# One access order for the products of a hybrid decoder trunk: parts and blocks of the tokens read in turn, with a PSUM layout to match

## The chip, the cores and the metric

The kernel runs on one core of a Trainium2 chip. The metric is the time of one execution in device microseconds; the kernel before takes 815.08 us, the median of three runs that lie between 813.9 and 815.81 us. A profile records one execution, instruction by instruction, on the engines of the core: TensorE (PE, with its weight loads listed apart as PEld), VectorE (DVE), ScalarE (ACT), GpSimd (POOL) and SyncE (SP), and the transfers of the DMA engines.

## The reference

Two layers work on 256 tokens of width 1024. Each layer normalises the stream, multiplies it by one wide input projection, runs three token mixers (a state-space scan, a sliding-window attention, a forgetting attention), gates and projects their outputs, merges them, and adds the result of an output projection to the stream. Cut to what matters here:

```python
for layer in range(DEPTH):
    h = rms_norm(x, norm_w[layer])                       # (256 tokens, 1024)
    proj = jnp.einsum('bsd,de->bse', h, w_in[layer])     # all branches from one projection
    (a_xbc, a_z, a_dt, b_q, b_k, b_v, b_z,
     c_q, c_k, c_v, c_f, c_z, gates) = jnp.split(proj, split_at, axis=-1)
    y_a = mamba2_branch(a_xbc, a_z, a_dt, ...)           # conv, scan, gate, group norm
    y_b = sliding_window_branch(b_q, b_k, b_v, b_z, ...)
    y_c = forgetting_attention_branch(c_q, c_k, c_v, c_f, c_z, ...)
    branch = jnp.einsum('bsiw,iwd->bsid', jnp.stack([y_a, y_b, y_c], axis=2), w_proj[layer])
    g = jax.nn.sigmoid(gates.reshape(b, s, N_BRANCH, d) + gate_bias[layer])
    x = x + jnp.einsum('bsd,de->bse', jnp.sum(g * branch, axis=2), w_out[layer])
return rms_norm(x, final_norm_w)
```

Everything is float32. The change touches how the columns of `proj` are computed that the kernel wants with channels on partitions: `a_xbc`, `a_z`, `b_q`, `b_k`, `b_z`, `c_q`, `c_k` and `c_z`.

## The kernel before, in words

**Two parts for each number.** TensorE multiplies values of a shortened float type (`F32R`). To keep float32 accuracy each operand is split into a high part, the value rounded to that type, and a low part, the rest. Weights arrive by DMA as parts of 1024 words a partition (`raw`), and `split` (L293 on ScalarE, L294 on VectorE) makes `hi` and `lo` of each. The tokens of a layer, normalised and transposed, are held in one tile `y.hT` of shape [128, 2, 2, 8, 128] (made in `both_streams`, L1226): the first 2 is the part `h` (high or low), the second is the block `a` of 128 tokens, then come the eight slices `k` of the width of 1024, then the 128 tokens `i` of a block. In words of four bytes, neighbouring tokens are 1 apart, the two blocks 1024 apart, the two parts 2048 apart. `y.hTh` and `y.hTl` are the high and the low part of it.

**The products that the change touches** are made by `both_sums`. It computes 128 channels by 256 tokens into `p`, one PSUM tile of 512 float32 columns (one of three with the name `mm`). For each of eight slices k there are two matmuls, both with weights as the stationary operand: the 512-wide product of the weights' high part with both parts of the tokens, and the 256-wide product of the weights' low part with the high part of the tokens. (The product of the two low parts is left out.) The first one writes columns 0 to 511: high tokens go to columns 0 to 255, low tokens to 256 to 511. The second one adds to columns 0 to 255. Within each half the two blocks of tokens alternate: token i of block a is column 2i + a. This order, which the kernel calls "in turn" (`tokens_in_turn`, `in_turn`), is used for the moving operand of every F32R matmul; where the weights are the moving operand (`tok`, `tok2`, `u_proj_normed`, with `dense`), the two halves of a row of weights alternate in the same way.

**After the products** the two halves of `p` have to be added, which also undoes the order (`ordered`, `halves`). `dma_sum` evicts both with ScalarE (L489, L490), and a DMA on GpSimd's queue (L491) adds one to the other in SBUF. `chan_sum` evicts the low half with ScalarE (L481) and adds the high half with VectorE (L482). There are 132 such calls: 84 `dma_sum` and 48 `chan_sum`.

**The order of the work** is written by a small planner at build time: `mm` adds an estimate for each matmul by its number of columns to a clock of its own, and `pump` uses this clock to decide where pieces of attention and scan are put between the products. The matmuls on TensorE then run in that written order. All matmuls are issued by one line, L109, and all transposes by L113, so groups are told apart by the names of tiles: `mm<-L,hi` is the 512-wide product of `both_sums` and `mm<-L,lo` the 256-wide one (L is a tile of tokens, hi and lo are the weights' parts), while `mm<-hi,L` and `mm<-lo,L` are the products in which the weights move.

Of the kernel before, what the change touches and what calls it, by code (L numbers as in the profile page):

```python
# [13 lines left out]
AF = mybir.ActivationFunctionType  # L14
ALU = mybir.AluOpType

P = 128
S = 256
# [32 lines left out]
def hybrid_trunk(  # L51
# [17 lines left out]
    def T(tag, shape, dtype=F32, bufs=None):  # L69
        count[0] += 1  # L70
        return sb.tile(shape, dtype, tag=tag, name=f"{tag}_{count[0]}",
                       bufs=bufs if bufs is not None else BUFS.get(tag, 1))

    def PS(tag, bufs):
        count[0] += 1
        return ps.tile([P, 512], F32, tag=tag, name=f"{tag}_{count[0]}", bufs=bufs)

    def pmm():
        return PS("mm", 3)

    def pmx():
        return PS("mx", 5)

    act = nc.scalar.activation
    stt = nc.vector.scalar_tensor_tensor
    tt = nc.vector.tensor_tensor
# [16 lines left out]
    def mm(o, a, b, **kw):  # L103
        n = b.free_size()
        if a.dtype == F32R:
            clock["t"] += max(0.094, n / 2350.0)
        else:
            clock["t"] += max(0.2, n / 587.0) * (0.5 if a.free_size() == 64 or a.shape[0] == 32 else 1.0)
        nc.tensor.matmul(o, a, b, **kw)  # L109
# [166 lines left out]
    def tokens_in_turn(a, k):  # L276
        return a[:, :, k, :].rearrange("p a i -> p i a")

    def ordered(ap):

        return ap.rearrange("p (i a) -> p a i", a=2)

    def halves(ap):

        return ap.rearrange("p (a i) -> p a i", a=2)
# [21 lines left out]
    def dense(pt, ah, al, bh, bl, w, mid=None):  # L307

        for k in range(NK):
            for i, (a, b) in enumerate(((ah, bh), (al, bh), (ah, bl))):  # L310
                mm(pt, a(k), b(k), start=(k == 0 and i == 0), stop=(k == NK - 1 and i == 2))
            if w.last and (k + 1) % w.kper == 0:
                release(w, k // w.kper + 1)
            if mid is not None and k == NK // 2 - 1:
                mid()
# [90 lines left out]
    def release(w, n):  # L406
        if n > w.released:
            state["held"] -= n - w.released
            w.released = n
            feed()  # L410
# [17 lines left out]
    for l in range(L):  # L428
        y = Layer()
# [36 lines left out]
            nc.gpsimd.tensor_copy(y.dsk[r, :], y.hb[r, 64:80].rearrange("p (j i) -> p i j", i=2)[:, i, :])  # L466


    def chan(y, w, c):

        p = pmm()
        dense(p[:, 0:S], lambda k: w.hi(k)[:, c:c + P], lambda k: w.lo(k)[:, c:c + P],
              lambda k: tokens_in_turn(y.hTh, k), lambda k: tokens_in_turn(y.hTl, k), w)
        return ordered(p[:, 0:S])

    def chan_sum(y, w, c, out):


        p = pmm()
        both_sums(y, w, c, p)  # L480
        finish(act(halves(out), ordered(p[:, S:2 * S]), AF.Copy))  # L481
        tt(halves(out), ordered(p[:, 0:S]), halves(out), op=ALU.add)  # L482

    def dma_sum(y, w, c, out):

        p = pmm()
        both_sums(y, w, c, p)
        lo = T("L1", [P, S])
        act(halves(lo), ordered(p[:, S:2 * S]), AF.Copy)  # L489
        last = act(halves(out), ordered(p[:, 0:S]), AF.Copy)  # L490
        nc.gpsimd.dma_start(out, lo, accum_op=ALU.add)  # L491
        finish(last)

# [2 lines left out]
        ends_later.append(f if n == 1 else lambda: after_evictions(n - 1, f))  # L496

    def both_sums(y, w, c, p):
        for k in range(NK):
            if k > 0:  # L500
                mm(p[:, 0:S], w.lo(k)[:, c:c + P], tokens_in_turn(y.hTh, k), start=False, stop=False)
            mm(p, w.hi(k)[:, c:c + P], y.hT[:, :, :, k, :].rearrange("p h a i -> p h i a"),
               start=(k == 0), stop=(k == NK - 1))
            if k == 0:
                mm(p[:, 0:S], w.lo(k)[:, c:c + P], tokens_in_turn(y.hTh, k), start=False, stop=False)
            if w.last and (k + 1) % w.kper == 0:
                release(w, k // w.kper + 1)

# [33 lines left out]
    def rotated(y, done):  # L542

        held = {}

        def u(half):
            def f(w):
                p = T("L1", [P, S])
                dma_sum(y, w, half * P, p)

                def turned():
                    for i in (half, 1 - half):
                        m = held[half, i] = T("L1", [P, S])
                        tt(m, p, cs[:, i, :], op=ALU.mult)
                    if half == 1:
                        done(held)
                after_evictions(3, turned)
                pump()
            return f
        return u(0), u(1)  # L560
# [253 lines left out]
    def u_conv(y, u, c):  # L814
        def f(w):
            if u == 8:
                y.bcT = T("L8", [P, 8, S])
            if u == 0:
                y.xs = T("L8", [P, 8, S])
            dst = y.xs[:, u, :] if u < 8 else y.bcT[:, u - 8, :]  # L820
            x_ = T("L1", [P, S])
            dma_sum(y, w, c, x_)

            def taps():
                a = T("L1", [P, S])
                act(a, x_, AF.Identity, scale=y.vec[:, 48 + u:49 + u], bias=y.vec[:, 64 + u:65 + u])  # L826
                for j in (2, 1, 0):
                    s = 3 - j
                    stt(a[:, s:S], x_[:, 0:S - s], y.vec[:, 16 * j + u:16 * j + u + 1], a[:, s:S],  # L829
                        op0=ALU.mult, op1=ALU.add)  # L830
                ends_later.append(lambda: end(a))

            def end(a):
                th = T("L1", [P, S])
                act(th, a, AF.Tanh)  # L835
                stt(dst, th, 1.0, a, op0=ALU.add, op1=ALU.mult)
                if u < 8 and u % 2 == 1:
                    launch(0, ssd_group(y, u // 2), D_G0)
            after_evictions(3, taps)
            pump()  # L840
        return f
# [4 lines left out]
    def finish(out):  # L846

        with tc.issue_after(out.ins):
            for _ in range(len(ends_later)):
                ends_later.pop(0)()  # L850
# [67 lines left out]
    def u_z(y, br, u, c):  # L918
        def f(w):
# [12 lines left out]
            if br == 1:  # L932
                dma_sum(y, w, c, o)
                after_evictions(3, gated)
                pump()
                return
            chan_sum(y, w, c, o)

            def normed():
# [88 lines left out]
    def u_ck(y, j, c):  # L1028
        def f(w):
            y.ckT[j] = T("qt", [P, 2, S])  # L1030
            (dma_sum if j < EARLY else chan_sum)(y, w, c, y.ckT[j][:, 0, :])
            if j % 2 == 0:
                launch(2, fox_quad(y, j), D_FOX)
            pump()
        return f

    def u_cq(y, j, c):
        def f(w):
            (dma_sum if j < EARLY else chan_sum)(y, w, c, y.ckT[j][:, 1, :])
            y.cqdone[j] = clock["t"] + (D_ADD if j < EARLY else 0.0)  # L1040
            pump()
        return f
# [210 lines left out]
    for y in layers:  # L1253
        l = y.l
        w = w_in[l]
# [149 lines left out]
    with tc.manual_schedule(engines={ENG.PE, ENG.DVE, ENG.Activation, ENG.Pool}):  # L1405
# [11 lines left out]
        p = pmx()  # L1417
# [93 lines left out]
        for i in range(2):  # L1511
# [6 lines left out]
                                op=ALU.add)  # L1518
# [50 lines left out]
```

## Time and profile before

| what | value |
|---|---|
| median of three runs | 815.08 us (813.9 to 815.81) |
| the profiled execution | 813.07 us, of which the span from first to last instruction is 811.4 us |
| granted TensorE clock | 0.998 of full speed |
| PE, matmuls in flight | 800.2 us, 99% of the span |
| DVE | 683.8 us, 84% |
| ACT | 533.4 us, 66% |
| POOL | 172.7 us, 21% |
| 512-wide products of `both_sums` | 1056 |
| 256-wide products of `both_sums` | 1056 |

How to read the views: a duration of a matmul is the time from its start until it has left the array, and matmuls overlap, so what one costs in a stream is the distance between the starts of two. The chain of waits follows the work that ended last back from the end; a row of it with "x72" is a run of 72 instructions on one engine, each of which waited for nothing but the one before it, and the time of such a row divided by its count is the cost of one. In a row of a group, the number of partitions and elements stands behind the names, then the count, the busy time, the mean duration in ns and the idle time of the engine ahead of it.

### The profile page before, as it was taken

The numbers are of one execution on the slowest core, as the hardware profiler recorded it, in microseconds if no ns is written. First come the engines' busy times: TensorE is split into PE (matmuls) and PEld (weight loads), VectorE is DVE, ScalarE is ACT, GpSimd is POOL, SyncE is SP. The second block draws the span as 40 slices with busy tenths as digits, with TensorE's granted clock in tenths as the row PEclk, the third lists the DMA queues.
The fourth block names the chain that finished last, engine by engine and source line by source line (L and its number), as shares of the span: only waits on it lengthen the run. The fifth ranks groups of instructions, "written<-read, shape, count | busy, mean of one in ns | idle before, by whom it ended". The sixth has DMA issues, their size and how long they took to land.

```text
span 811.4 us, 14867 instructions
## 1 busy us (share of the span) xinstructions
PE 800.2 (99%) x5178; PEld 714.2 (88%) x5178; DVE 683.8 (84%) x1412; ACT 533.4 (66%) x1142; POOL 172.7 (21%) x227
## 2 busy tenths in 40 slices
PE   8999999999999999999999999999999999999996
PEld 8998988888888888888998899888888988888896
DVE  6869999978998998776775799999879989869865
ACT  7777767865875785543565678677747677745452
POOL 3167113130321000130001741122313410002000
PEclk9999999999999999999999999999999999999999
DMA  9998888699675565667688987689986645566632
GB/s 311 279 262 183 240 221 203 197 261 252 175 211 163 164 191 180 211 208 246 214 261 259 241 209 220 159 214 257 272 253 175 212 130 160 172 228 218 210 106 77
DMA packets 139418, 170.43 MB, mean 210 GB/s; under 512 B 9976, under 2 KB 107072, under 8 KB 139344
## 3 DMA queue, kind: packets, MB, share of 16 engines
q1 hardware_dynamic: 114960, 140.53, 55.9%
q0 software_dynamic: 12928, 12.68, 9.8%
q10 hardware_dynamic: 11456, 16.28, 7.1%
q8 instruction: 41, 0.67, 0.3%
q14 instruction: 33, 0.27, 0.1%
HBM read 154.71 MB, written 2.16 MB: 193 GB/s over the span
## 4 chain that ended last, share of the span: by engine, by line
PE 96%; DMA 2%; DVE 1%; ACT 1%; issue 0%; SPq 0%; DVEq 0%
PE mm L109 83%; PE mx L109 10%; PE mx L113 3%; DMA raw<-in_w_in_dram 1%; DMA raw<-in_w_proj_dram 1%; DMA hb<-in_sinks_dram 0%; DVE lo L294 0%; ACT L L695 0%; ACT hi L293 0%; SPq L363 0%; SPq L189 0%; DVE L L1431 0%; DVE L L1127 0%; DVE L L1128 0%; ACT L L1435 0%
## 5 line engine op out<-in xcount | busy, mean ns | idle before, releaser
L109 PE MATMUL mm<-L,hi 128*128 128x512 f32 x1056 | 354.6, 387 | 0.3
L294 DVE TENSOR_TENSOR lo<-raw,hi 128x1024 fp32r<-128x1024 f32 (+1 forms) x276 | 313.1, 1153 | 37.8 <-ACT hi L293 36.6
L109 PE MATMUL mm<-hi,L 128*128 128x512 f32 (+2 forms) x1168 | 303.3, 349 | 0.1
L293 ACT ACTIVATE hi<-raw 128x1024 fp32r<-128x1024 f32 (+1 forms) x276 | 265.6, 981 | 51.1 <-PE mm L109 37.1
L109 PE MATMUL mm<-L,lo 128*128 128x256 f32 x1056 | 266.6, 273 | 0.0
L109 PEld LDWEIGHTS mm<-hi,L 128*128 128x128 f32 x1168 | 206.0, 190 | 22.6 <-issue 1.0
L109 PEld LDWEIGHTS mm<-L,hi 128*128 128x128 f32 x1056 | 195.2, 190 | 28.0 <-issue 5.2
L109 PEld LDWEIGHTS mm<-L,lo 128*128 128x128 f32 x1056 | 202.1, 191 | 5.3
L109 PE MATMUL mm<-lo,L 128*128 128x512 f32 (+2 forms) x584 | 201.5, 347 | 0.0
L109 PEld LDWEIGHTS mm<-lo,L 128*128 128x128 f32 x584 | 110.2, 190 | 10.7
L491 POOL DMA_DIRECT2D L<-L x68 | 60.1, 908 | 198.2 <-ACT L L490 153.8
L1057 POOL TENSOR_SCALAR_AFFINE_SELECT bias<-bias 128x128 f32<-128x128 f32 x64 | 40.7, 671 | 69.3 <-DMA bias<-cumd 69.2
L829 DVE SCALAR_TENSOR_TENSOR L<-L,vec,L 128x255 f32<-128x255 f32 (+2 forms) x96 | 46.2, 481 | 2.1 <-ACT L L826 0.3
L489 ACT ACTIVATE L<-mm 128x256 f32<-128x256 f32 x84 | 32.1, 382 | 19.1 <-PE mm L109 15.6
L1091 ACT ACTIVATE L<-L 128x512 f32<-128x512 f32 x24 | 15.1, 631 | 39.9 <-DVE L L1088 31.7
L655 ACT ACTIVATE pp<-pp,nm 128x128 f32<-128x128 f32 x64 | 28.2, 442 | 18.3 <-DVE nm L649 18.3
L613 ACT ACTIVATE pp<-pp,nm 128x128 f32<-128x128 f32 x32 | 12.6, 394 | 25.1 <-DVE nm L618 24.4
L1088 DVE TENSOR_TENSOR L<-mm,L 128x512 f32<-128x512 f32 x22 | 15.1, 686 | 16.4 <-DMA L<-in_gate_bias_dram 8.8
L491 POOL DMA_DIRECT2D qt<-L x16 | 13.8, 860 | 70.9 <-ACT qt L490 69.4
L1124 POOL TENSOR_TENSOR L<-L,L 128x512 f32<-128x512 f32 x8 | 12.8, 1600 | 68.0 <-DVE L L1123 46.2
L490 ACT ACTIVATE L<-mm 128x256 f32<-128x256 f32 x68 | 26.3, 386 | 1.5 <-DMA L<-L 1.5
L835 ACT ACTIVATE L<-L 128x256 f32<-128x256 f32 x32 | 13.4, 418 | 19.0 <-DVE L L829 18.9
(210 smaller groups left out, 913.7 us busy)
## 6 DMA issues: line engine op xcount, KB each, us to landing
raw<-in_w_in_dram SPq DMA_DIRECT2D x191, 512.0 KB, 5.3
raw<-in_w_proj_dram SPq DMA_DIRECT2D x48, 512.0 KB, 5.6
L<-L POOLq DMA_DIRECT2D x72, 128.0 KB, 5.1
raw<-in_w_out_dram SPq DMA_DIRECT2D x16, 512.0 KB, 4.8
bias<-cumd ACTq DMA_DIRECT2D x16, 256.0 KB, 3.7
L<-cumd ACTq DMA_DIRECT2D x8, 512.0 KB, 5.4
L<-in_gate_bias_dram ACTq DMA_DIRECT2D x12, 256.0 KB, 6.2
qt<-L POOLq DMA_DIRECT2D x16, 128.0 KB, 5.5
```

The lines of the kernel that those rows point to most:

```text
L109: nc.tensor.matmul(o, a, b, **kw)
L113: nc.tensor.transpose(o, a, i)
L293: keep(act)(hi, src, AF.Copy)
L294: keep(tt)(lo, src, hi.bitcast(F32), op=ALU.subtract)
L489: act(halves(lo), ordered(p[:, S:2 * S]), AF.Copy)
L490: last = act(halves(out), ordered(p[:, 0:S]), AF.Copy)
L491: nc.gpsimd.dma_start(out, lo, accum_op=ALU.add)
L655: act(pp[:, i, sl], pp[:, i, sl], AF.Exp, scale=-1.0, bias=nm[:, e:e + 1], accum_out=sums[:, e:e + 1])
L829: stt(a[:, s:S], x_[:, 0:S - s], y.vec[:, 16 * j + u:16 * j + u + 1], a[:, s:S], op0=ALU.mult, op1=ALU.add)
L1057: nc.gpsimd.affine_select(out=bias[:, i, dst], in_=bias[:, i, src], compare_op=ALU.is_ge, fill=NEG, base=0, pattern=[[-1, P]], channel_mul ...
L1088: tt(halves(g), p, halves(y.gb), op=ALU.add)
L1091: finish(act(g, g, AF.Tanh, scale=0.5))
```

## The change

The 512-wide product reads the tokens in another order and so fills PSUM in another order. Before, it walks part, then token, then block (h, i, a): three nested steps. Now it walks token, then part and block together (i, then h and a), and since the part step of 2048 words is twice the block step of 1024, the four (h, a) combinations are one step of 1024 words taken four times: two nested steps. Token i of block a in part h is now column 4i + 2h + a of `p`. The 256-wide product reads what it read, and its result has to be added to the columns of the high part: it now writes columns 4i and 4i + 1, skips 4i + 2 and 4i + 3, and so on (`own`). The evictions read every fourth column, where they read every second one (`streams` in place of `ordered`). An unused function (`chan`) goes. Count, sizes and order of the instructions are the same, and so are the planner's estimates, which depend on the number of columns alone.

```diff
-    def chan(y, w, c):
...
-        return ordered(p[:, 0:S])
+    def streams(p):
+
+        return p.rearrange("p (i h a) -> p h a i", h=2, a=2)
 
     def chan_sum(y, w, c, out):
         p = pmm()
         both_sums(y, w, c, p)
-        finish(act(halves(out), ordered(p[:, S:2 * S]), AF.Copy))
-        tt(halves(out), ordered(p[:, 0:S]), halves(out), op=ALU.add)
+        q = streams(p)
+        finish(act(halves(out), q[:, 1, :, :], AF.Copy))
+        tt(halves(out), q[:, 0, :, :], halves(out), op=ALU.add)
 
     def dma_sum(y, w, c, out):
         p = pmm()
         both_sums(y, w, c, p)
         lo = T("L1", [P, S])
-        act(halves(lo), ordered(p[:, S:2 * S]), AF.Copy)
-        last = act(halves(out), ordered(p[:, 0:S]), AF.Copy)
+        q = streams(p)
+        act(halves(lo), q[:, 1, :, :], AF.Copy)
+        last = act(halves(out), q[:, 0, :, :], AF.Copy)
         nc.gpsimd.dma_start(out, lo, accum_op=ALU.add)
         finish(last)
 
     def both_sums(y, w, c, p):
+        own = p.rearrange("p (i h a) -> p i h a", h=2, a=2)[:, :, 0, :]
         for k in range(NK):
             if k > 0:
-                mm(p[:, 0:S], w.lo(k)[:, c:c + P], tokens_in_turn(y.hTh, k), start=False, stop=False)
-            mm(p, w.hi(k)[:, c:c + P], y.hT[:, :, :, k, :].rearrange("p h a i -> p h i a"),
+                mm(own, w.lo(k)[:, c:c + P], tokens_in_turn(y.hTh, k), start=False, stop=False)
+            mm(p, w.hi(k)[:, c:c + P], y.hT[:, :, :, k, :].rearrange("p h a i -> p i (h a)"),
                start=(k == 0), stop=(k == NK - 1))
             if k == 0:
-                mm(p[:, 0:S], w.lo(k)[:, c:c + P], tokens_in_turn(y.hTh, k), start=False, stop=False)
+                mm(own, w.lo(k)[:, c:c + P], tokens_in_turn(y.hTh, k), start=False, stop=False)
```

More of the change, by code (lines that the diff above doesn't have):

```diff
@@ L466, in layer_vec @@
             nc.gpsimd.tensor_copy(y.dsk[r, :], y.hb[r, 64:80].rearrange("p (j i) -> p i j", i=2)[:, i, :])
-    def chan(y, w, c):
-        p = pmm()
-        dense(p[:, 0:S], lambda k: w.hi(k)[:, c:c + P], lambda k: w.lo(k)[:, c:c + P],
-              lambda k: tokens_in_turn(y.hTh, k), lambda k: tokens_in_turn(y.hTl, k), w)
-        return ordered(p[:, 0:S])
+    def streams(p):
+        return p.rearrange("p (i h a) -> p h a i", h=2, a=2)
     def chan_sum(y, w, c, out):
```

## The prediction

> **What bounds the kernel now.** I read the page first, then the groups by shape, then the chain of waits, and last TensorE's instructions one by one. The page, and from the groups by shape the two products of `both_sums` and a transpose:
>
> ```profile
> span 811.4 us, 14867 instructions
> PE 800.2 (99%) x5178; PEld 714.2 (88%) x5178; DVE 683.8 (84%) x1412; ACT 533.4 (66%) x1142; POOL 172.7 (21%) x227
> PEclk9999999999999999999999999999999999999999
> PE 96%; DMA 2%; DVE 1%; ACT 1%; issue 0%; SPq 0%; DVEq 0%
> ```
>
> ```profile
> L109 PE MATMUL mm<-L,hi 128*128 128x512 f32 x1056 | 354.6, 387 | 0.3
> L109 PE MATMUL mm<-L,lo 128*128 128x256 f32 x1056 | 266.6, 273 | 0.0
> L113 PE MATMUL mx<-ident,L 128*128 128x128 f32 x98 | 15.1, 286 | 1.3 <-DVE L L1128 1.2
> ```
>
> TensorE has work in 99% of the span, at full clock throughout, and 96% of the chain that ended last is on it. Ahead of the 1056 wide products it sat idle for 0.3 us in all. So the time is a sum of matmul costs, and a nanosecond on each of 1056 matmuls is about one microsecond of the kernel. Durations don't tell that cost, because matmuls overlap (387 + 273 ns is twice what a pair takes, as the next rows show). The chain has runs in which TensorE waits for nothing:
>
> ```profile
> 221.84 5.24 PE mm L109 x32
> 767.38 15.54 PE mm L109 x72
> 782.93 0.44 PE mx L113 x4
> ```
>
> What these runs are made of is told by TensorE's instructions in the windows 222.0 to 227.0 and 767.5 to 782.8:
>
> ```profile
> L109 PE MATMUL mm<-L,hi x16: 379/382/463, 221.6 to 226.7; 128*128 128x512 f32 x16
> L109 PE MATMUL mm<-L,lo x16: 272/273/275, 221.9 to 226.6; 128*128 128x256 f32 x16
> L109 PE MATMUL mm<-hi,L x48: 379/379/462, 767.1 to 782.3; 128*128 128x512 f32 x48
> L109 PE MATMUL mm<-lo,L x24: 379/379/379, 767.7 to 782.5; 128*128 128x512 f32 x24
> ```
>
> The first run is two calls of `both_sums`: 16 pairs in 5.24 us, 327.5 ns a pair. The second run is 72 products 512 wide in which the weights move: 15.54 / 72 = 215.8 ns each. The third is four transposes of 128 columns, 110 ns each. How a pair divides is seen in the timeline of TensorE, whose first column is the start:
>
> ```profile
> 222.11 0.38 PE L109 MATMUL mm<-L,hi 128*128 128x512 f32 x1
> 222.33 0.27 PE L109 MATMUL mm<-L,lo 128*128 128x256 f32 x1
> 222.44 0.38 PE L109 MATMUL mm<-L,hi 128*128 128x512 f32 x1
> 222.66 0.27 PE L109 MATMUL mm<-L,lo 128*128 128x256 f32 x1
> 222.77 0.38 PE L109 MATMUL mm<-L,hi 128*128 128x512 f32 x1
> 222.99 0.27 PE L109 MATMUL mm<-L,lo 128*128 128x256 f32 x1
> 223.10 0.38 PE L109 MATMUL mm<-L,hi 128*128 128x512 f32 x1
> 223.31 0.27 PE L109 MATMUL mm<-L,lo 128*128 128x256 f32 x1
> 223.42 0.38 PE L109 MATMUL mm<-L,hi 128*128 128x512 f32 x1
> ```
>
> From 222.11 to 223.42 are four pairs; the wide product holds the array for 0.22 + 0.22 + 0.22 + 0.21 = 0.87 us, 218 ns each, the narrow one for 0.44 us, 110 ns each. So the wide product, whose operand is read with three nested steps, takes 218 ns where one of the same width with two nested steps takes 215.8: 2.2 ns more. The median durations, 382 against 379 ns, differ the same way. Everything that the change can gain on TensorE lies in these 2.2 ns.
>
> **The change part by part.** No instruction is removed, added or moved, no queue gets a DMA more, and no wait changes: the evictions still need the last product of their tile, and in `chan_sum` VectorE still reads what ScalarE wrote. There are four edits with a price.
>
> *The wide product's read*, 1056 times. It now has two nested steps, like the products of 767 us. If the third step is what costs 2.2 ns, it falls to 215.8 ns: 1056 x 2.2 = 2.3 us. What isn't in the trace is a read from four places in turn; every F32R product here reads from two. Bounds: from below, 215.8 ns, since no 512-wide product here is faster. From above, the nearest row of a product that takes longer for a column is the transpose: 110 ns for 128 columns, 0.86 ns a column against 215.8 / 512 = 0.42, so 440 ns for 512 columns, (440 - 218) x 1056 = +234 us. I take 215.8, because the row it is nearest to reads from two places 1 KB apart, and the narrow product, with its two places 4 KB apart, runs at 110 / 256 = 0.43 ns a column as well: a switch of place at every column, and the distance, show no cost here.
>
> [...]
>
> *The narrow product's write*, 1056 times. It now writes two adjacent columns, skips two, and so on. No matmul of the trace writes with gaps that could be timed. Bounds: 110 ns, as now, and from above the transpose's rate again, 0.86 x 256 = 220 ns: (220 - 110) x 1056 = +116 us. A gain is excluded, as it reads the same operand and has the same columns to deliver. I take 110 ns: pairs stay adjacent, and two columns take 0.86 ns whether or not the next two are skipped, if PSUM is written by pairs.
>
> [...]
>
> *The evictions' read*, 264 times. They go from a step of 8 bytes to one of 16. The rows of the tile `mm` and, for comparison, of the groups by shape:
>
> ```profile
> L489 ACT ACTIVATE L<-mm x84: 360/384/436, 42.1 to 612.2; 128x256 f32<-128x256 f32 x84
> L490 ACT ACTIVATE L<-mm x68: 368/378/447, 42.4 to 578.6; 128x256 f32<-128x256 f32 x68
> L490 ACT ACTIVATE qt<-mm x16: 365/379/407, 158.7 to 612.5; 128x256 f32<-128x256 f32 x16
> L481 ACT ACTIVATE L<-mm x32: 358/367/391, 216.3 to 696.4; 128x256 f32<-128x256 f32 x32
> L481 ACT ACTIVATE qt<-mm x16: 359/366/385, 222.2 to 657.6; 128x256 f32<-128x256 f32 x16
> L482 DVE TENSOR_TENSOR L<-mm,L x32: 408/416/419, 217.5 to 697.7; 128x256 f32<-128x256 f32 x32
> L482 DVE TENSOR_TENSOR qt<-mm,qt x16: 407/410/424, 223.0 to 658.5; 128x256 f32<-128x256 f32 x16
> ```
>
> ```profile
> L536 ACT ACTIVATE bias<-mm 128x256 f32<-128x256 f32 x2 | 0.8, 375 | 0.2 <-PE mm L109 0.2
> L1401 ACT ACTIVATE cs<-mx 32x256 f32<-32x256 f32 x8 | 3.0, 374 | 0.1
> L1019 ACT ACTIVATE L<-mm 128x512 f32<-128x512 f32 x2 | 1.2, 592 | 4.6 <-PE mx L113 4.6
> L695 ACT ACTIVATE L<-mx 128x512 f32<-128x512 f32 x24 | 13.6, 591 | 5.0 <-PE mx L109 4.3 <-PE mx L113 0.7
> ```
>
> L536 and L1019 read every second column, L1401 and L695 adjacent ones: 375 against 374 ns, 592 against 591. A step of 8 bytes costs ScalarE nothing, so I take nothing for 16. The upper bound is one more element time for each: (591 - 374) / 256 = 0.85 ns, +217 ns on 256 columns: 216 on ScalarE, 47 us busy more, and 48 on VectorE, 10.4 us. What covers that is the engines' slack in the stages concerned:
>
> ```profile
> 200.00:240.00 40.00, 40.00 (x295) 35.92 (x295) 38.27 (x108) 29.70 (x74) 11.80 (x18) 1.00 0.68 187
> 219.00:227.00 8.00, 8.00 (x52) 7.21 (x50) 8.00 (x13) 6.67 (x12) 4.65 (x8) 1.00 0.76 231
> ```
>
> The columns behind the length are PE, PEld, DVE, ACT and POOL. ScalarE has 10 us of 40 free; VectorE, which does the sums of `chan_sum` here, has 1.7 us, and in the 8 us around two such calls none at all. So on ScalarE the cost would be hidden, and on VectorE it would come through, up to 10.4 us in all. A third edit's price, then: nothing, at most 10.4 us.
>
> *Planner and `chan`*: nothing, since the estimates go by the number of columns, and `chan` is called by no one.
>
> **The sum.** -2.3 us on TensorE. Of it 96%, the chain's share, reaches the end: -2.2 us. VectorE's 1.7 us of slack in the 40 us above is more than TensorE's gain there, so it isn't what takes over: 295 matmuls in 40 us can hold at most 40 / 0.3275 = 122 pairs, a gain of 0.27 us. Against the profiled execution: 813.07 - 2.2 = 810.9 us. That execution lies 2.0 us under the median of the three runs, so against the median: 815.08 - 2.2 = 812.9 us.
>
> **The rivals.**
>
> [...]
>
> *The gaps in the write cost* (slower). If PSUM takes the narrow product's pairs at half the rate: 815.1 - 2.2 + 116 = 929 us. For it: nothing here writes so. Against it: the pairs stay whole.
>
> *A few ns on read, write or eviction* (slower, by little). Up to 10.4 us from VectorE as above, or some 3 to 10 ns on one of the products: 816 to 826 us.
>
> *The change doesn't do what it does on paper* (no change). The 2.2 ns may belong to the jump between the two parts, 8 KB, or to reading 8 KB apart at all, and stay; or the write's second nested step costs the narrow product what the read's third did the wide one. Then 815.1 us. For it: the wide product is the only one with either property, so the trace can't part them.
>
> **How the numbers follow.** Changes of up to 0.2%, 1.6 us, can't be told from none by a measurement of this kernel. Forecast: 0.45, of which 0.05 would measure under that bound, since 2.2 us is only 0.27%. No effect: 0.12. A few ns: 0.10. The write at half rate: 0.13. The read at half rate: 0.20. So faster 0.40, the same 0.05 + 0.12 = 0.17, slower 0.43. The likeliest case's own range is 811.5 (2.3 us under the lowest run, 813.9) to 814.5 us. The range that holds 0.80 takes in all but the slow read: 811.5 to 929 us.
>
> **What would show it.** Right: in a run of pairs on the chain 325.3 ns a pair, that is 5.20 us for 32 matmuls, with the wide product's median duration at 379 ns and the narrow one's at 273; evictions within 10 ns of the rows above. Wrong by the read: starts after the wide product more than 218 ns apart. Wrong by the write: starts after the narrow one more than 110 ns apart. Wrong by the evictions: L481, L482, L489 or L490 longer by 100 ns or more, with TensorE idle ahead of L109 on VectorE or ScalarE.

## The result, and the profile after

The changed kernel takes 874.86 us (median; 874.71 to 875.36) against 814.49 us for the kernel before on the same chip: a ratio of 1.0756, with a 95% interval of 1.0742 to 1.0771. It is 60 us slower, where 2.2 us faster was forecast.

The page of the changed kernel, and of its groups by shape the two products of `both_sums` and the products in which the weights move:

```profile
span 873.0 us, 14867 instructions
PE 862.2 (99%) x5178; PEld 715.5 (82%) x5178; DVE 688.3 (79%) x1412; ACT 539.8 (62%) x1142; POOL 171.1 (20%) x227
PEclk9999999999999999999999999999999999999999
PE 98%; DMA 1%; DVE 0%; ACT 0%; SPq 0%; issue 0%; DVEq 0%
```

```profile
L109 PE MATMUL mm<-L,hi 128*128 128x512 f32 x1056 | 416.5, 446 | 0.0
L109 PE MATMUL mm<-L,lo 128*128 128x256 f32 x1056 | 267.9, 274 | 0.0
L109 PE MATMUL mm<-hi,L 128*128 128x512 f32 x800 | 239.4, 381 | 0.0
```

Count of instructions (14867) and granted clock (0.998) are those of before, and TensorE is still busy in 99% of the span. One group has changed: the wide product lasts 446 ns in the mean, where it was 387. The narrow one is at 274 (273), the products in which the weights move at 381, as they were. What a pair costs is told by the chain of waits and by TensorE's timeline:

```profile
230.98 6.20 PE mm L109 x32
829.03 15.54 PE mm L109 x72
```

```profile
231.31 0.44 PE L109 MATMUL mm<-L,hi 128*128 128x512 f32 x1
231.59 0.27 PE L109 MATMUL mm<-L,lo 128*128 128x256 f32 x1
231.70 0.45 PE L109 MATMUL mm<-L,hi 128*128 128x512 f32 x1
231.98 0.28 PE L109 MATMUL mm<-L,lo 128*128 128x256 f32 x1
232.10 0.44 PE L109 MATMUL mm<-L,hi 128*128 128x512 f32 x1
232.37 0.27 PE L109 MATMUL mm<-L,lo 128*128 128x256 f32 x1
232.48 0.43 PE L109 MATMUL mm<-L,hi 128*128 128x512 f32 x1
232.75 0.27 PE L109 MATMUL mm<-L,lo 128*128 128x256 f32 x1
232.87 0.44 PE L109 MATMUL mm<-L,hi 128*128 128x512 f32 x1
```

Sixteen pairs take 6.20 us, 387.5 ns each, 60 ns more than before; 1056 x 60 = 63 us, and the span grew by 873.0 - 811.4 = 61.6 us. In the four pairs of the timeline the wide product holds the array for 0.28 + 0.28 + 0.27 + 0.27 = 1.10 us, 275 ns each. The 72 products 512 wide in which the weights move still take 15.54 us. So nearly the whole loss is in one kind of instruction. Summed over the two traces, the distances from the start of a wide product to the next start grew from 238.4 to 298.2 us, and those of the narrow products from 115.6 to 117.4 us: together the 61.6 us of the span. Over all 1056 pairs that is 58.3 ns each, a little less than in this run.

### The profile page after: what moved, and what is told of

It is laid out like the page before. It is cut to its first block, busy times and chain, and to the rows that moved or that the text cites. A ratio compares the mean times of both kernels' runs of the same rounds, so it can differ in the third digit from the quotient of the medians.

```text
span 873.0 us, 14867 instructions
## 1 busy us (share of the span) xinstructions
PE 862.2 (99%) x5178; PEld 715.5 (82%) x5178; DVE 688.3 (79%) x1412; ACT 539.8 (62%) x1142; POOL 171.1 (20%) x227
## 4 chain that ended last, share of the span: by engine, by line
PE 98%; DMA 1%; DVE 0%; ACT 0%; SPq 0%; issue 0%; DVEq 0%
PE mm L109 86%; PE mx L109 9%; PE mx L113 3%; DMA raw<-in_w_in_dram 1%; ACT L L695 0%; SPq L363 0%; SPq L189 0%; DVE L L1431 0%; DVE L L1128 0%; ACT L L1435 0%; ACT hi L1444 0%; ACT L L1212 0%; DVE L L1187 0%; DVE L L1191 0%; DVE L L288 0%
## 5 line engine op out<-in xcount | busy, mean ns | idle before, releaser
L109 PE MATMUL mm<-L,hi 128*128 128x512 f32 x1056 | 416.5, 446 | 0.0
L490 POOL DMA_DIRECT2D L<-L x68 | 60.7, 905 | 225.6 <-ACT L L489 134.8
L1057 POOL TENSOR_SCALAR_AFFINE_SELECT bias<-bias 128x128 f32<-128x128 f32 x64 | 44.0, 755 | 85.9 <-DMA bias<-cumd 82.9
L655 ACT ACTIVATE pp<-pp,nm 128x128 f32<-128x128 f32 x64 | 28.2, 443 | 18.5 <-DVE nm L649 18.5
L490 POOL DMA_DIRECT2D qt<-L x16 | 13.8, 860 | 87.0 <-ACT qt L489 76.0
L489 ACT ACTIVATE L<-mm 128x256 f32<-128x256 f32 x68 | 25.8, 379 | 0.0
L930 DVE SCALAR_TENSOR_TENSOR L<-L,L 128x256 f32<-128x256 f32 x48 | 20.7, 435 | 5.6 <-ACT L L929 5.5
L969 POOL TENSOR_TENSOR sm<-sm,mhalf 128x8 f32<-128x8 f32 x2 | 3.4, 1682 | 107.3 <-DVE sm L968 107.3
```

Source lines behind the costliest of these rows:

```text
L489: last = act(halves(out), q[:, 0, :, :], AF.Copy)
L655: act(pp[:, i, sl], pp[:, i, sl], AF.Exp, scale=-1.0, bias=nm[:, e:e + 1], accum_out=sums[:, e:e + 1])
L930: stt(o, th, 1.0, o, op0=ALU.add, op1=ALU.mult)
L1057: nc.gpsimd.affine_select(out=bias[:, i, dst], in_=bias[:, i, src], compare_op=ALU.is_ge, fill=NEG, base=0, pattern=[[-1, P]], channel_mul ...
```

## The experiments

### Is it the read or the PSUM layout?

The change has two halves, and they can be had one at a time, because a matmul's output can be written in an order other than that of its input, as in the next two kernels. In the first run the read is as before and the layout is the changed one; in the second it is the other way round.

```diff
-            mm(p, w.hi(k)[:, c:c + P], y.hT[:, :, :, k, :].rearrange("p h a i -> p i (h a)"),
+            mm(p.rearrange("p (i h a) -> p h i a", h=2, a=2), w.hi(k)[:, c:c + P],
+               y.hT[:, :, :, k, :].rearrange("p h a i -> p h i a"),
```

> The wide product reads as before (part, token, block: two places in turn), but all three writers and readers of PSUM use the changed layout: it writes column pairs with a gap of two columns, the narrow product too, the evictions read every fourth column. Theory 'four places in the read' (the wide product's 276 instead of 218 ns come from reading four places in turn): 218 ns again, the narrow product at 111 ns as in the changed kernel, 814.5 + 1056 x 1.5 ns = 816 us. Rival 'layout' (the changed PSUM layout makes the products slow): 860 us or more, with starts after the wide product about 276 ns apart, since now the wide product has the gaps as well.

```diff
-            mm(p, w.hi(k)[:, c:c + P], y.hT[:, :, :, k, :].rearrange("p h a i -> p h i a"),
+            mm(p.rearrange("p (h i a) -> p i h a", h=2, a=2), w.hi(k)[:, c:c + P],
+               y.hT[:, :, :, k, :].rearrange("p h a i -> p i h a"),
```

> The wide product reads in the changed order (token, then part and block: four places in turn), but its output is written to the columns of before, so that it jumps 256 columns after each pair; the narrow product and the evictions are those of before. Theory 'four places in the read': 276 ns after the wide product, 110 ns after the narrow one, about 873 us (1.6 us less than the changed kernel). Rival 'layout': 218 ns, about 815 us. If the jumps between pairs cost as well, more than 276 ns.

The layout alone: 813.06 us, 1.0002 of the kernel before (0.9993 to 1.0011). The read alone: 873.58 us, 1.0748 (1.0734 to 1.0762). The runs of 16 pairs on the chain, first of the kernel with the changed layout, then of the one with the changed read:

```profile
154.58 5.24 PE mm L109 x32
```

```profile
230.48 6.19 PE mm L109 x32
```

327.5 and 387 ns a pair: the read carries all of it, and the layout nothing, although in the first of these kernels the wide product too writes pairs with gaps. The first expectation had put 1.5 ns on each narrow product down to its write, 1.6 us in all; the layout alone shows no such growth (813.06 us against 812.75 before). From a narrow product to the wide one behind it the trace of the kernel before has 109.5 ns in the mean, that of the changed kernel 111.1. The durations of the narrow products say where these 1.6 ns belong: their median is 273 ns and their longest 275 before and with the layout alone, 274 and 279 with the read alone and in the changed kernel. So the growth goes with the read as well. The evictions of the kernel with the changed layout, which read every fourth column, from the tile `mm`:

```profile
L489 ACT ACTIVATE L<-mm x68: 370/378/447, 42.5 to 579.7; 128x256 f32<-128x256 f32 x68
L479 ACT ACTIVATE L<-mm x32: 358/367/390, 216.4 to 697.0; 128x256 f32<-128x256 f32 x32
L480 DVE TENSOR_TENSOR L<-mm,L x32: 407/414/419, 217.6 to 698.4; 128x256 f32<-128x256 f32 x32
```

Medians of 378, 367 and 414 ns stand against 378, 367 and 416 for every second column. (The edit shifts the lines: L489 here is what L490 was, L479 and L480 are what L481 and L482 were.)

### Is it the distance between the places?

```diff
-        y.hT = T("L16", [P, 2, 2, NK, P], F32R)
+        y.hT = T("L16", [P, NK, 2, 2, P], F32R).rearrange("p k h a i -> p h a k i")
```

> The changed kernel, with the tokens stored so that the four places of a read lie 512 bytes apart in place of 4 KB (slice k outermost, then part, block, token). Theory 'four places in the read', whatever their distance: 276 ns, 875 us. Rival 'distance' (places a multiple of 4 KB apart get in each other's way): 216 to 218 ns, 813 to 816 us. Anything between would say that the distance matters in part.

873.78 us, 1.0752 (1.0738 to 1.0766), and the same pairs:

```profile
231.05 6.20 PE mm L109 x32
```

Four places 512 bytes apart cost what four places 4 KB apart cost, 387.5 ns a pair.

### Was there a gain to be had from the third step?

```diff
-        y.hT = T("L16", [P, 2, 2, NK, P], F32R)
-        y.normal = tuple(y.hT[:, i, :, :, :] for i in range(2))
+        y.hT = T("L16", [P, 2, NK, 2, P], F32R)
+        y.normal = tuple(y.hT[:, :, :, i, :] for i in range(2))
...
-            mm(p, w.hi(k)[:, c:c + P], y.hT[:, :, :, k, :].rearrange("p h a i -> p h i a"),
+            mm(p, w.hi(k)[:, c:c + P], y.hT[:, :, k, :, :].rearrange("p a h i -> p (h i) a"),
```

> The kernel before, with the tokens stored block, slice, part, token, so that for one slice part and token are one run of 256 adjacent words: the wide product reads the columns in the very order of before, with two nested steps in place of three, from two places 8 KB apart. PSUM layout, narrow product and evictions are those of before. Theory 'the third nested step costs 2.2 ns': starts 215.8 ns apart, 814.5 - 2.2 = 812.3 us. Rival 'the 2.2 ns belong to something else in the wide product': 218 ns, 814.5 us.

812.53 us, 1.0003 (0.9993 to 1.0013): no change. The pairs of the chain stay as they were:

```profile
154.25 5.24 PE mm L109 x32
```

327.5 ns with two nested steps as with three. The 2.2 ns by which the wide product exceeds other products of its width aren't the price of the third step. The trace of the kernel before shows what they go with. Most wide products stand behind a narrow one, but the first wide product of a call can stand right behind the last one of the call ahead. Here is one of either kind out of the run at 221.84 us, from the windows 223.92 to 223.96 and 224.47 to 224.50:

```profile
L109 PE MATMUL mm<-L,hi x1: 382/382/382, 223.8 to 223.8; 128*128 128x512 f32 x1
L109 PE MATMUL mm<-L,hi x1: 379/379/379, 224.3 to 224.3; 128*128 128x512 f32 x1
```

Behind a narrow product 382 ns, behind a wide one 379, with the same three nested steps. By the starts in the trace, 902 of the 924 wide products behind a narrow one have the next start 218 or 219 ns later, and 64 of the 68 behind a wide one 215 or 216 ns later. The narrow products, which have two nested steps, do the same: 111 or 112 ns behind another narrow one, 109 or 110 behind a wide one. So the 2.2 ns belong to the order of narrow and wide products; why, no run shows.

### How does the cost depend on the order of the words?

Four places cost 57 ns in 512 columns (275 against 218), where the forecast had no cost and the transpose's rate 222 ns (440 against 218). On 1296 products 57 ns are 74 us, which makes 887 us. No row of the traces gives this price, so I varied the order in which a product reads. Seven kernels leave `both_sums` as before and change the 1296 products of 512 columns in which the weights move, by a switch on the width in `in_turn`; each run has one of the lines shown, and the comments name it. `ordered` and `halves` follow, but for the two runs with places 16 and 8 bytes apart, whose results stay in the order of the read. (In the expectations a line is 16 adjacent bytes, four words.) The eighth kernel varies the changed one; there the narrow product, `streams` and the evictions follow the line shown.

```diff
     def in_turn(ap):
+        if ap.shape[-1] == 512:
+            return ap                                        # one place
+            return ap.rearrange("p (a i) -> p i a", a=8)     # eight places
+            return ap.rearrange("p (i a) -> p a i", a=4)     # every fourth word
         return ap.rearrange("p (a i) -> p i a", a=2)
```

> The kernel before, with the 1296 products of 512 columns in which the weights move reading their 512 words one after another (one place), PSUM and evictions to match. [...] Rival 'only two in turn is fast' (adjacent words in turn are slow too): towards the transpose's rate, 440 ns, 1296 x 224 ns = 290 us more, 1100 us.

> The kernel before, with the same 1296 products reading from eight places 256 bytes apart in turn instead of two 1 KB apart. [...] Rival 'a price for each round' (each wrap of the innermost step costs): eight places have half the rounds of four, 29 ns a product, 850 us. Rival 'a price that grows with the places': more than 887 us.

> The kernel before, with the same 1296 products reading every fourth word of a row of weights, then again from the next word: one place, but every column lies 16 bytes behind the one before it, and a line comes back only after 128 columns. PSUM has blocks of 128 columns, and the evictions spread them by four in SBUF. [...] Rival 'places' (the number of separate runs counts, not the lines): 215.8 ns, 813 us.

```diff
-            mm(p, w.hi(k)[:, c:c + P], y.hT[:, :, :, k, :].rearrange("p h a i -> p i (h a)"),
+            mm(p, w.hi(k)[:, c:c + P], y.hT[:, :, :, k, :].rearrange("p h a (i j) -> p i (h a) j", j=2),
```

> The changed kernel, but each of the places gives two adjacent tokens before the next place follows: the wide product reads pairs from four places, the narrow one pairs from two, PSUM has pairs of tokens in the order of the places, and the evictions read pairs 32 bytes apart. [...] Rival 'places': 276 ns, about 875 us. If adjacent words in turn are slow, longer than that, and the narrow product too.

The four took 831.16, 1163.32, 1127.11 and 1120.41 us. In the first three the same run of 72 products that took 15.54 us before stands on the chain, in the order one place, eight places, every fourth word:

```profile
783.41 16.76 PE mm L109 x72
```

```profile
1085.22 35.21 PE mm L109 x72
```

```profile
1051.99 33.12 PE mm L109 x72
```

That is 233, 489 and 460 ns a product. In the kernel with pairs, a run of 16 pairs of products, and its timeline:

```profile
216.68 9.95 PE mm L109 x32
```

```profile
217.91 0.63 PE L109 MATMUL mm<-L,hi 128*128 128x512 f32 x1
218.35 0.36 PE L109 MATMUL mm<-L,lo 128*128 128x256 f32 x1
218.53 0.63 PE L109 MATMUL mm<-L,hi 128*128 128x512 f32 x1
218.97 0.36 PE L109 MATMUL mm<-L,lo 128*128 128x256 f32 x1
219.15 0.63 PE L109 MATMUL mm<-L,hi 128*128 128x512 f32 x1
```

The wide product takes 440 ns, the narrow one 180. The number of places alone doesn't order these times: eight cost far more than four (489 against 275 ns; so the price for each round, 29 ns a product, falls, and one that grows with the places holds for these two); every fourth word of one row costs 460 ns; and pairs from four places, which change the place half as often as single words do, are slower than those (440 against 275 ns). One regularity covers all of them: take the even and the odd columns apart. With two places in turn the even columns are adjacent words of one place, the odd ones of the other, and four of each lie in 16 bytes. One place read in order leaves two in 16 bytes for either; every fourth word leaves one. Four places give either half two places to switch between, eight places and pairs from four places give it four. I called this regularity "two paths" and had it foretell three more orders; a fourth run asks whether four places cost the weights what they cost the tokens:

```diff
     def in_turn(ap):
+        if ap.shape[-1] == 512:
+            return ap.rearrange("p (i a) -> p a i", a=2)              # every second word
+            return ap.rearrange("p (o a j) -> p o j a", a=2, j=4)     # two places, 16 bytes apart
+            return ap.rearrange("p (o a j) -> p o j a", a=2, j=2)     # two places, 8 bytes apart
+            return ap.rearrange("p (a i) -> p i a", a=4)              # four places
         return ap.rearrange("p (a i) -> p i a", a=2)
```

> The kernel before, with the 1296 products of 512 columns in which the weights move reading every second word of a row of weights, then the words left out: one place, 8 bytes from column to column. Theory 'two paths' (even and odd columns are fetched apart, and each of the two is quick as long as it stays within 16 bytes; in the runs so far a product took 216 ns where each path had four columns in such a line, 231 where it had two, 460 where it had one): each path now steps by 16 bytes, one column a line, 460 ns, about 1127 us. Rival 'one path' (only the step from a column to the next counts): two columns a line, as much more than 231 ns as the lines per column double, 231 to 250 ns, 831 to 857 us.

> The same products read from two places that lie only 16 bytes apart, a column from each in turn, four from each before both move on by 32 bytes (words 0, 4, 1, 5, 2, 6, 3, 7, then 8, 12 and so on). Their results are left in this order, so that gates, values and projections are mixed up among columns and the output is not the reference's; the work is the same. Theory 'two paths': each path has four columns in its line, 216 ns, 813 us. Rival 'places' (what counts is that the two runs are far apart): as one place, 231 ns, 831 us.

> As the run with two places 16 bytes apart, but 8 bytes: words 0, 2, 1, 3, then 4, 6 and so on; the results are left in this order too. Theory 'two paths': each path has two columns in a line of 16 bytes, as when words are read one after another: 231 ns, 831 us. Rival 'in turn' (it is enough that neighbouring columns aren't neighbours in memory): 216 ns, 813 us.

> The same products read from four places 512 bytes apart in turn, results in order. By the products of the changed kernel, 276 ns: 1296 x 60 = 78 us more, 891 us. If four places in turn cost weights less or more than tokens, the change's price depends on what else TensorE reads, not on the places alone.

They took 1117.98, 811.41, 831.22 and 891.09 us; the run of 72 products in each, in that order:

```profile
1043.92 32.62 PE mm L109 x72
```

```profile
765.65 15.54 PE mm L109 x72
```

```profile
783.26 16.76 PE mm L109 x72
```

```profile
837.27 20.25 PE mm L109 x72
```

All products of 512 columns together; a path is the even or the odd columns, and its places and its columns in 16 bytes are counted from the order of the words:

| order of the read | places for each path | columns of a path in 16 bytes | ns |
|---|---|---|---|
| two places in turn (before), also 16 bytes apart | 1 | 4 | 216 |
| one place, also two places 8 bytes apart | 1 | 2 | 233 |
| every second word; every fourth word | 1 | 1 | 453; 460 |
| four places, weights; tokens (the change) | 2 | 4 | 281; 275 |
| pairs from two places (an estimate: 180 for 256 columns, doubled) | 2 | 2 | 360 |
| pairs from four places | 4 | 2 | 440 |
| eight places | 4 | 4 | 489 |

The two runs that differ only in 16 against 8 bytes (216 against 233 ns) and the step of two words (453) are what the rivals got wrong: they had 231 to 250 ns for the step of two words, 231 ns for two places 16 bytes apart, and 216 ns for 8 bytes. Of the orders tried, the shortest time goes only with those in which even columns and odd columns each walk through adjacent words, four at a time or more (216 ns). The two paths are my model of the times above, worked out from the first runs (216, 233, 460 ns); no run shows that even and odd columns are fetched apart, as my expectation words it. The model foretold three runs to within 2% (460, 216 and 231 ns against 453, 216 and 233). The fourth was expected from the changed kernel's price (276 ns, measured 281). What happens when a path has two places (275 ns, neither 216 nor 453) was measured, not foretold, and is not explained.

## Why the prediction was wrong

**What bounds the kernel.** Right: a sum of matmul costs with nothing idle; 60 ns on 1056 products came out as 60 us.

**The wide product's read.** This is the step that failed: "I take 215.8, because the row it is nearest to reads from two places 1 KB apart". It took 275 ns, inside the bounds of 215.8 and 440 ns, and the run with the read alone shows that the read is what costs it. The sentence under it, that "a switch of place at every column, and the distance, show no cost here", was true of the rows and still no ground for four places. Counted by even and odd columns, two places in turn leave one place to each (216 ns), four in turn leave two (275 ns); why the second takes longer, no run shows. The read at half rate, which the chances gave 0.20, was right in kind. Its price, the bound of +234 us, was about four times the real one (60 us).

**The third nested step.** Wrong as well: with the read's places left at two and the step taken away, the wide product didn't get quicker. The forecast gain of 2.3 us wasn't there. The rival that the change doesn't do what it does on paper said that the 2.2 ns may belong to something else, but looked for it in the 8 KB between the parts and held that the trace can't part the causes. It can: 379 ns, the shortest of the 16 wide products in the prediction's own row (379/382/463), is the one that stands behind another wide product.

**The narrow product's write.** Right: no cost, which the run with the layout alone shows (327.5 ns a pair). The sign set for it, starts more than 110 ns apart behind the narrow product, came all the same (111.1 ns), but with the read: the narrow product's longest duration is 279 ns with the read alone, as in the changed kernel, and 275 with the layout alone. That PSUM is written by pairs, on which the forecast took its 110 ns, was the author's assumption and isn't shown: no run breaks the pairs. What the runs show is that pairs with a gap of two columns cost nothing.

**The evictions' read.** Right: a step of 16 bytes costs ScalarE and VectorE nothing (378 against 378, 414 against 416 ns).

**The chances.** The measured time is inside the range by luck: the range reached to 929 us for the sake of the write, which cost nothing, and was meant to leave the slow read out. That the read would be slow had a chance of 0.20. (The lower end, 2.3 us under 813.9, is 811.6 and not 811.5; nothing hangs on it.)

## What to carry to other kernels

Where a rate holds for two of something, the trace doesn't say that it holds for four; ask what of the pattern the two may fit, and price the next one by measuring it. For `F32R` products read so that even columns and odd columns each run through adjacent words (two runs in turn, 216 to 218 ns, whether 16 bytes or 1, 4 or 8 KB apart), and don't trade that for fewer nested steps. A PSUM layout of adjacent pairs with gaps, and evictions of every fourth column, cost nothing in these runs (813.06 us against 812.75) and can be had without touching the read, by scattering the output.

## What the runs showed of the hardware that was not expected

- A 512-wide `F32R` product that reads 512 words in order takes 233 ns, and one that reads two runs in turn 216. The simplest order is 8% slower.
- The price of an order spans more than a factor of two for the same 512 words: from 216 ns to 453 for every second word and 489 for eight places in turn.
- Pairs of adjacent words from four places (440 ns) are slower than single words from four places (275 ns).
- A wide product that scatters its output, even with a jump of 256 columns after each pair, takes no longer than one that writes in order: in the run with the read alone 387 ns a pair, 387.5 in the changed kernel.
- A product right behind a 256-wide one takes 2 to 3 ns longer than behind a 512-wide one: 218 against 216 ns for the wide product, 112 against 109 ns for the narrow one, with the same read.
